# A hybrid decoder layer on one core: 19 instead of 12 of the 22 gate and up pairs by Strassen's products, and the decay differences made by ACT instead of POOL

## The chip, the core and the metric

The kernel runs on one core of one Trainium2 chip. Its engines work beside each other, each through its own list of instructions in the order in which they stand: TensorE (PE, with its weight loads shown apart as PEld), VectorE (DVE), ScalarE (ACT), GpSimd (POOL), and SyncE (SP), which here only issues DMAs. An instruction that waits for another engine or for a DMA holds up everything that stands behind it on its own engine. The metric is the time of one execution on the device in microseconds (us); lower is better. Three executions of the kernel before took 1591.46, 1591.48 and 1591.81 us; the median is 1591.48 us.

## What is computed

One decoder layer on 512 tokens of width 1024, in float32. The reference, cut to what the change touches:

```python
def swiglu(u, w_gate_up, w_down):
    gate, up = jnp.split(u @ w_gate_up, 2, axis=-1)
    return (jax.nn.silu(gate) * up) @ w_down

# per layer
h = h + 0.5 * swiglu(rmsnorm(h, ffn1_norm), ffn1_w_gate_up, ffn1_w_down)      # D_FF = 2816
...                       # short convolution, Mamba-2 SSD, gates, cross attention
h = h + 0.5 * swiglu(rmsnorm(h, ffn2_norm), ffn2_w_gate_up, ffn2_w_down)

# in the SSD part, per group of 8 heads and per chunk of 128 tokens
seg = acs[..., :, None] - acs[..., None, :]            # acs: running sum of dt * a
decay = jnp.exp(jnp.where(causal, seg, -jnp.inf))
y_diag = jnp.einsum('bcgls,bcgkls,bcsgkp->bclgkp', cb, decay, x)
```

## The kernel before

**Number format.** A matmul operand is kept as two parts that PE can multiply, `hi` (a rounded copy, made by ACT, line 103) and `lo` (what is left over, made by DVE, line 104). A product of two such operands is three matmuls for each 128 rows of the inner dimension: hi by hi, lo of the activations, lo of the weights. The third of every three matmuls therefore reads the weights' `lo`.

**The two feed-forward parts.** `ffn` runs at the start of the layer and again at its end. Its 2816 gate and 2816 up columns make 22 pairs `ct` = 0 to 21: 128 gate columns and 128 up columns each, with 1 MB of weights. They are worked off in blocks of eight (pairs 0 to 7, 8 to 15, 16 to 21). After each block come eight down projections (`job`, lines 130 to 132), one for each 128 columns of the model's width; these take the block's results `s` as their operands.

A pair is made in one of two ways. `plain` does 48 matmuls of 512 columns. The other way takes the pair as a 2 by 2 block product (gate and up against the two halves of the inner dimension, the two halves of the tokens on the other side) and does it with Strassen's seven products instead of eight: 84 matmuls of 256 columns. It needs sums of weight blocks, made anew for each pair, and sums of token blocks (`token_sums`, tiles `tq`, `th`, `tl`), made once in each of the two parts, behind pair 1. Which way a pair goes is decided by `seven(ct)`, line 47: before, for 4, 5, 7, 8, 10, 11, 13, 14, 16, 17, 19 and 20, so that never more than two such pairs follow one another.

Such a pair has a first half, `seven_a`, and a second, `seven_b`. `seven_a(n + 1)` is written ahead of `seven_b(n)`, so PE does first half, first half, second half, first half, second half, and so on. In `seven_a` the weights arrive in two transfers, `ca` (tile `wr`, three buffers) and `db` (two buffers). DVE adds blocks into `sa` (lines 278, 279), into `wr` itself (282) and `sb` (285); ACT and DVE split `sa` into `wh`, `wl` and the changed `wr` into `xh`, `xl` (two buffers). PE does four products: two from `sa` into the psum tile B, two from `wr` into A. ACT and DVE then copy and add halves of B (lines 290, 291) and of A (294, 295) into `ev`. In `seven_b` the split `sb` gives one product, the split `db` two; then DVE puts the results together (306, 307, 311, 312), ACT does the silu (247), DVE the product (251), and both split it into `sh`, `sl` for the down projections. A buffer of `db` is free for the transfer of the pair after next when its own split has been made (`xl<-db`, line 104).

**The SSD part.** For each of 32 heads a tile `m` (128 by 512) is filled by a DMA that repeats one head's row of `acs` on all partitions; then comes the difference with the column of `acs`, clamped on one side (lines 522 to 525), `exp` (526), and DVE's product with `cb` (527). PE takes it in line 539. Two heads at a time make one step of `ssd_out`.

**What sets the order.** The code is written in the order above, and a scheduler in the building of the program then puts each engine's instructions into one fixed order, so that an edit at one place can move instructions elsewhere. That order is what the engines follow.

Of the kernel before, what the change touches and what calls it, by code (L numbers as in the profile page):

```python
# [22 lines left out]
AF = mybir.ActivationFunctionType  # L23
ALU = mybir.AluOpType
AX = mybir.AxisListType

P = 128
# [14 lines left out]
NC = 4  # L42
# [3 lines left out]

def seven(ct):

    return ct >= 4 and ct % 3 != 0


COL = {}
# [10 lines left out]
def layer(ctx: ExitStack, tc: tile.TileContext, a, out):  # L63
    nc = tc.nc
    V, S, G, TE = nc.vector, nc.scalar, nc.gpsimd, nc.tensor
# [15 lines left out]
    def ps(tag="pj"):  # L81
        return psp.tile([P, T], F32, tag=tag, name=nm(tag), bufs=PJ if tag == "pj" else 8 - PJ)
# [16 lines left out]
    def pc(name, i):  # L99
        return prm[:, COL[name] + i:COL[name] + i + 1]  # L100
# [87 lines left out]
    def ffn(gname, wgu, wd, fin=None):  # L188
# [126 lines left out]
        for b0 in range(0, KF, SB):  # L315
            b1 = min(KF, b0 + SB)
            wait = None
            for ct in range(b0, b1):
                if seven(ct):
                    nxt = seven_a(ct)  # L320
                    if wait is not None:
                        seven_b(*wait)
                    wait = nxt
                else:
                    p = plain(ct)
                    if ct == 0:
                        r = rms(h, D, wk)
                    plain_out(ct, *p)
                    if wait is not None:
                        seven_b(*wait)  # L330
                        wait = None
                if ct == 1:
                    token_sums()
# [37 lines left out]
    def proj(ct):  # L371
        p = ps()
        job(p, win[ct], u)
        return p
# [9 lines left out]
    with tc.tile_pool(name="mx", bufs=1, reuse_waits="tile") as mx:  # L384

        def mt(tag, bufs, shape=(P, T), dt=F32):
            return mx.tile(list(shape), dt, tag=tag, name=nm(tag), bufs=bufs)
# [7 lines left out]
        for c in range(NC):  # L395
# [4 lines left out]
        dt, acs, dte, eend = (keep[:, i, :] for i in range(4))  # L400
# [3 lines left out]
                        in0=ptr[:, 0:P].rearrange("p (c h) -> p h c", c=NC),  # L404
                        in1=dtb[:, 0, :].rearrange("p (h c) -> p h c", c=NC), op=ALU.add)
# [107 lines left out]
        def ssd_out(g, ct, xs, cb, xdt, prev):  # L513
            yg = []
            for i in range(4):
                h0 = 8 * g + 2 * i
                ms = []
                for hh in range(2):
                    m = mt("m", MB)
                    DQ.dma_start(out=m, in_=acd_h[h0 + hh].partition_broadcast(P))  # L520
                    m4 = m.rearrange("p (c l) -> p c l", c=NC)
                    G.tensor_tensor(out=m4, in0=m4,
                                    in1=acs[:, (h0 + hh) * NC:(h0 + hh + 1) * NC].unsqueeze(2)
                                    .to_broadcast([P, NC, P]), op=ALU.subtract)
                    S.activation(out=m, in_=m, func=AF.Relu, scale=-1.0)
                    S.activation(out=m, in_=m, func=AF.Exp, scale=-1.0)
                    V.tensor_tensor(out=m, in0=m, in1=cb, op=ALU.mult)
                    ms.append(m)
                ea = mt("ea", 2)
                for hh in range(2):  # L530
                    DQ.dma_start(out=ea[64 * hh:64 * hh + 64, :],
                                 in_=acd_h[h0 + hh].partition_broadcast(64))
                S.activation(out=ea, in_=ea, func=AF.Exp)
                yd = ps("ss")
                for c in range(NC):
                    cs = slice(c * P, (c + 1) * P)
                    for hh in range(2):
                        q0 = (2 * i + hh) * 64
                        TE.matmul(yd[64 * hh:64 * hh + 64, cs], xdt[c][:, q0:q0 + 64], ms[hh][:, cs],  # L539
                                  start=True, stop=True)  # L540
                yo = ps("ss")
                for c in range(1, NC):
                    cs = slice(c * P, (c + 1) * P)
                    TE.matmul(yo[:, cs], prev[c - 1][:, i * P:(i + 1) * P], ct[:, cs],
                              start=True, stop=True)
                V.tensor_tensor(out=ea[:, P:], in0=yo[:, P:], in1=ea[:, P:], op=ALU.mult)
                y = mt("yg", 4)
                V.scalar_tensor_tensor(out=y, in0=xs[i], scalar=pc("ssm_d", 4 * g + i), in1=yd,
                                       op0=ALU.mult, op1=ALU.add)
                V.tensor_tensor(out=y[:, P:], in0=y[:, P:], in1=ea[:, P:], op=ALU.add)  # L550
                yg.append(y)
            return yg
# [16 lines left out]
        for g in range(NG):  # L569
            bt, ct, xs = nxt  # L570
            cb, xdt, prev = ssd_state(g, bt, ct, xs)
            yn = norm_y(g, ssd_out(g, ct, xs, cb, xdt, prev), zs)
            if g < NG - 1:
                nxt = ssd_in(g + 1)
                zs = gate_z(g + 1)
            else:
                sgb = []
                for k in range(KD):
                    p = proj(72 + k)
                    t = mt("xs", 8)  # L580
                    V.tensor_tensor(out=t, in0=p, in1=r, op=ALU.mult)
                    S.activation(out=t, in_=t, func=AF.Sigmoid)
                    sgb.append(t)
            for k in range(KD):
                p = ps()
                job(p, a["w_os"][k][:, g * 512:(g + 1) * 512], yn)
                if g == 0:
                    S.copy(out=yb[k], in_=p)
                else:
                    V.tensor_tensor(out=yb[k], in0=p, in1=yb[k], op=ALU.add)  # L590
                if g == NG - 1:
                    V.tensor_tensor(out=yb[k], in0=yb[k], in1=sgb[k], op=ALU.mult)

    with tc.tile_pool(name="mb", bufs=1, reuse_waits="tile") as mb:
        def wt(tag, bufs, dt=F32):
            return mb.tile([P, T], dt, tag=tag, name=nm(tag), bufs=bufs)
# [14 lines left out]
        for k in range(KD):  # L611
            pcg, pv, pb = proj(8 + k), proj(16 + k), proj(k)
            c = wt("c", 2)
# [29 lines left out]
        for k in range(KD):  # L643
            p = ps()
# [5 lines left out]
    with tc.tile_pool(name="xa", bufs=1, reuse_waits="tile") as xa:  # L650
        kT, vm = [], []
        with tc.tile_pool(name="xn", bufs=1, reuse_waits="tile") as xm:
# [6 lines left out]
            for k in range(KD):  # L659
                p = ps()  # L660
# [26 lines left out]
        with tc.tile_pool(name="xo", bufs=1, reuse_waits="tile") as xo:  # L687
# [86 lines left out]
            for k in range(KD):  # L774
                p = ps()
# [142 lines left out]
```

## Time and profile before

| | |
|---|---|
| median of three executions | 1591.48 us |
| the profiled execution, as timed | 1592.54 us |
| its span in the profile | 1590.8 us |
| instructions in the span | 20744 |
| PE, DVE, ACT, POOL busy, share of the span | 98%, 66%, 46%, 3% |

The profiled execution took 1.06 us more than the median; 1.7 us of it lie outside the span. The page gives each engine's busy time, the span in 40 slices, the chain of work that ended last, and groups of instructions by line. A matmul's duration in it is modelled and overlaps the next, so what a matmul costs is read from the distance between two starts. In a row of the timeline the columns are the start, the duration, the engine, the line, the operation, what it writes and reads, and in brackets the idle time before it and what ended that.

### The profile page before, as it was taken

To read this page: it belongs to the slowest core of one execution; us is meant where nothing else is said; L and a number is where in the kernel's file an instruction comes from. 1 tells how busy PE (TensorE), PEld (TensorE's weight loads), DVE (VectorE), ACT (ScalarE), POOL (GpSimd) and SP (SyncE) were. 2 spreads that over 40 slices of the span, in tenths; PEclk is the share of its full clock that TensorE was granted. 3 is DMA by queue.
4 is the path that set the end of the run, shared out by engine and by line. 5 is a ranking of instruction groups with operands and counts; after the bars stand their busy time and mean duration, and the time that the engine had idled before them with its cause. 6 is when DMAs were issued, how large, how long until landed. Compare 5 with 4: busy or idle time off the path is not lost.

```text
span 1590.8 us, 20744 instructions
## 1 busy us (share of the span) xinstructions
PE 1557.4 (98%) x8253; PEld 1318.0 (83%) x8253; DVE 1056.0 (66%) x1502; ACT 733.7 (46%) x1008; POOL 52.7 (3%) x54
## 2 busy tenths in 40 slices
PE   7999999999989999899999999999999999999997
PEld 6888988987778777787888888888888898998986
DVE  6856856777684877958565544565556876666765
ACT  7432433445768593765332233344344642342343
POOL 0000000002020200201000000000000000000000
PEclk9999999999999999999999999999999999999999
DMA  5432333245242423323242322235204233233221
GB/s 196 133 93 93 98 112 100 66 132 188 93 133 80 138 75 117 122 93 108 78 146 93 105 94 93 95 105 185 93 27 130 83 120 107 93 95 111 86 62 71
DMA packets 53920, 168.70 MB, mean 106 GB/s; under 512 B 6320, under 2 KB 6832, under 8 KB 53824
## 3 DMA queue, kind: packets, MB, share of 16 engines
q1 hardware_dynamic: 51952, 161.03, 31.8%
q0 software_dynamic: 1584, 5.31, 0.9%
q8 instruction: 64, 1.05, 0.3%
q10 hardware_dynamic: 288, 1.05, 0.2%
q14 instruction: 32, 0.26, 0.1%
HBM read 163.10 MB, written 4.26 MB: 105 GB/s over the span
## 4 chain that ended last, share of the span: by engine, by line
PE 55%; DVE 2%; issue 1%; ACT 1%; DMA 0%; DVEq 0%; ACTq 0%
PE pj L132 12%; PE pj L131 12%; PE pj L130 12%; PE pj L212 5%; PE pj L214 5%; PE pj L215 5%; DMA ea<-acd 0%; PE pj L676 0%; PE pj L678 0%; PE pj L677 0%; PE ss L539 0%; DVE wl L104 0%; PE ss L758 0%; ACT wh L103 0%; PE ss L721 0%
## 5 line engine op out<-in xcount | busy, mean ns | idle before, releaser
L103 ACT CAST wh<-wr 128x1024 fp32r<-128x1024 f32 (+2 forms) x250 | 243.6, 975 | 479.9 <-PE pj L131 332.2
L104 DVE TENSOR_TENSOR wl<-wr,wh 128x1024 fp32r<-128x1024 f32 (+2 forms) x250 | 282.0, 1129 | 112.6 <-ACT wh L103 111.0
L130 PE MATMUL pj<-uh,wh 128*128 128x512 f32 (+1 forms) x712 | 281.2, 395 | 0.0
L132 PE MATMUL pj<-uh,wl 128*128 128x512 f32 (+1 forms) x712 | 280.4, 394 | 0.0
L131 PE MATMUL pj<-ul,wh 128*128 128x512 f32 (+1 forms) x712 | 279.5, 393 | 0.0
L212 PE MATMUL pj<-uh,wh 128*128 128x512 f32 (+1 forms) x416 | 153.3, 369 | 8.3 <-ACT wh L103 7.1
L132 PEld LDWEIGHTS pj<-uh,wl 128*128 128x128 f32 (+1 forms) x712 | 133.9, 188 | 29.0 <-issue 0.7
L130 PEld LDWEIGHTS pj<-uh,wh 128*128 128x128 f32 (+1 forms) x712 | 133.8, 188 | 28.6 <-issue 0.9
L131 PEld LDWEIGHTS pj<-ul,wh 128*128 128x128 f32 (+1 forms) x712 | 134.0, 188 | 27.8
L214 PE MATMUL pj<-ul,wh 128*128 128x512 f32 (+1 forms) x416 | 152.4, 367 | 0.0
L215 PE MATMUL pj<-uh,wl 128*128 128x512 f32 (+1 forms) x416 | 151.9, 366 | 0.0
L130 PE MATMUL pj<-sh,wh 128*128 128x512 f32 x346 | 135.3, 391 | 0.1
L131 PE MATMUL pj<-sl,wh 128*128 128x512 f32 x346 | 135.1, 390 | 0.2
L132 PE MATMUL pj<-sh,wl 128*128 128x512 f32 x346 | 134.8, 390 | 0.0
L212 PEld LDWEIGHTS pj<-uh,wh 128*128 128x128 f32 x416 | 78.6, 189 | 22.6 <-ACT wh L103 7.1
L214 PEld LDWEIGHTS pj<-ul,wh 128*128 128x128 f32 x416 | 79.0, 190 | 13.1 <-DVE ul L140 0.5
L215 PEld LDWEIGHTS pj<-uh,wl 128*128 128x128 f32 x416 | 78.5, 189 | 12.8 <-DVE wl L104 0.2
L131 PEld LDWEIGHTS pj<-sl,wh 128*128 128x128 f32 x346 | 65.0, 188 | 14.5 <-DVE sl L104 1.5
L130 PEld LDWEIGHTS pj<-sh,wh 128*128 128x128 f32 x346 | 65.0, 188 | 14.0 <-ACT sh L103 0.9
L132 PEld LDWEIGHTS pj<-sh,wl 128*128 128x128 f32 x346 | 65.0, 188 | 13.4
L352 DVE SCALAR_TENSOR_TENSOR dn<-pj,r 128x512 f32<-128x512 f32 x47 | 32.4, 690 | 57.2 <-PE pj L132 56.9
L381 DVE SCALAR_TENSOR_TENSOR cv<-cx,prm,cv 128x511 f32<-128x511 f32 (+2 forms) x72 | 62.1, 866 | 3.4 <-ACT cv L378 3.1
(278 smaller groups left out, 3088.6 us busy)
## 6 DMA issues: line engine op xcount, KB each, us to landing
wr<-in_w_in SPq DMA_DIRECT2D x80, 512.0 KB, 3.2
wr<-in_w_gu SPq DMA_DIRECT2D x63, 512.0 KB, 3.8
wr<-in_w_d SPq DMA_DIRECT2D x32, 512.0 KB, 3.5
db<-in_w_gu SPq DMA_DIRECT2D x24, 512.0 KB, 3.8
m<-acd SPq DMA_DIRECT2D x32, 256.0 KB, 3.9
wr<-in_w_os SPq DMA_DIRECT2D x32, 256.0 KB, 3.1
wr<-in_w_d SPq DMA_DIRECT2D x16, 384.0 KB, 3.2
ea<-acd SPq DMA_DIRECT2D x32, 128.0 KB, 4.4
```

Of the source, the lines that this page charges most:

```text
L103: S.copy(out=hi, in_=src)
L104: V.tensor_tensor(out=lo, in0=src, in1=hi, op=ALU.subtract)
L130: TE.matmul(pt, hi[:, s_], xh, start=(k == 0), stop=False)
L131: TE.matmul(pt, hi[:, s_], xl, start=False, stop=False)
L132: TE.matmul(pt, lo[:, s_], xh, start=False, stop=(k == nk - 1))
L212: TE.matmul(pt, hi[:, c], xh, start=start and k == 0, stop=False, skip_group_check=True)
L214: TE.matmul(pt, hi[:, c], xl, start=False, stop=False, skip_group_check=True)
L215: TE.matmul(pt, lo[:, c], xh, start=False, stop=stop and k == 3, skip_group_check=True)
L352: V.scalar_tensor_tensor(out=dn, in0=pd, scalar=0.5, in1=r, op0=ALU.mult, op1=ALU.mult)
L381: V.scalar_tensor_tensor(out=acc[:, d:], in0=x[:, :T - d], scalar=pc(wname, j0 + j), in1=acc[:, d:], op0=ALU.mult, op1=ALU.add)
```

## The change

```diff
-    return ct >= 4 and ct % 3 != 0
+    return ct >= 3
...
                     DQ.dma_start(out=m, in_=acd_h[h0 + hh].partition_broadcast(P))
-                    m4 = m.rearrange("p (c l) -> p c l", c=NC)
-                    G.tensor_tensor(out=m4, in0=m4,
-                                    in1=acs[:, (h0 + hh) * NC:(h0 + hh + 1) * NC].unsqueeze(2)
-                                    .to_broadcast([P, NC, P]), op=ALU.subtract)
-                    S.activation(out=m, in_=m, func=AF.Relu, scale=-1.0)
+                    for c in range(NC):
+                        col = (h0 + hh) * NC + c
+                        S.activation(out=m[:, c * P:(c + 1) * P], in_=m[:, c * P:(c + 1) * P],
+                                     func=AF.Relu, scale=-1.0, bias=acs[:, col:col + 1])
                     S.activation(out=m, in_=m, func=AF.Exp, scale=-1.0)
```

In each of the two feed-forward parts, pairs 3, 6, 9, 12, 15, 18 and 21 go over to the block products: 38 pairs in all instead of 24. Behind the plain pairs 0, 1 and 2 no plain pair is left, and the block products now come in unbroken rows of 5, 8 and 6 pairs. The second edit does the difference inside the activation, by its bias, in four instructions of 128 columns each; POOL does no arithmetic in the SSD part any more. Lines behind 522 stand one lower in the changed file.

The first place is on DVE, in the first feed-forward part, where the token sums end and the first block products begin. It is one piece of the difference (`tq`, `tl` are token sums; `wr_89`, `wr_92` are the weights of pair 3 before, `wr_87`, `db_88` those of pair 3 now, `wr_98`, `db_99` those of pair 4 before; `pj_76`, `pj_77` the psum tiles of plain pair 2).

```order
 L238 SCALAR_TENSOR_TENSOR tq_73_364<-tq_73_364,ug_72_361 128x256
-L104 TENSOR_TENSOR wl_91_447<-wr_89_445,wh_90_446 128x1024
-L104 TENSOR_TENSOR wl_94_477<-wr_92_475,wh_93_476 128x1024
+L278 TENSOR_TENSOR sa_89_447<-wr_87_443,db_88_444 128x512
+L279 TENSOR_TENSOR sa_89_447<-wr_87_443 128x512
 L104 TENSOR_TENSOR tl_75_370<-tq_73_364,th_74_369 128x1024
-L278 TENSOR_TENSOR sa_100_517<-wr_98_513,db_99_514 128x512
+L282 TENSOR_TENSOR wr_87_443<-wr_87_443,sa_89_447 128x512
+L104 TENSOR_TENSOR wl_91_451<-sa_89_447,wh_90_450 128x1024
 L268 TENSOR_TENSOR gt_84_435<-pj_77_374,r_41_241 128x512
```

Where DVE split the weights of plain pair 3 it now makes the sums of a block-product pair.

The second place is also on DVE, in the second block of the first feed-forward part. Before, from the split of pair 10's `db` (tile `db_237`) on; `ev_257`, `xl_280` belong to pair 11, `wl_273` to plain pair 12, `sa_287`, `db_286` to pair 13, `sa_298` to pair 14, `xx_262` to pair 10:

```order
L104 TENSOR_TENSOR xl_261_1592<-db_237_1442,xh_260_1591 128x2x512
L295 TENSOR_TENSOR ev_246_1485<-pj_244_1459,ev_246_1485 128x256
L306 TENSOR_TENSOR xx_262_1631<-ev_246_1485 128x256
L104 TENSOR_TENSOR wl_273_1677<-wr_271_1675,wh_272_1676 128x1024
L291 TENSOR_TENSOR ev_257_1558<-pj_256_1533,ev_257_1558 128x256
L278 TENSOR_TENSOR sa_287_1773<-wr_285_1769,db_286_1770 128x512
L279 TENSOR_TENSOR sa_298_1846<-wr_296_1842 128x512
L282 TENSOR_TENSOR wr_285_1769<-wr_285_1769,sa_287_1773 128x512
L295 TENSOR_TENSOR ev_257_1558<-pj_255_1532,ev_257_1558 128x256
L104 TENSOR_TENSOR xl_280_1718<-db_248_1515,xh_279_1717 128x2x512
L307 TENSOR_TENSOR xx_262_1631<-pj_245_1460,ev_246_1485 128x512
```

In the change, from the row ahead of the split of pair 10's `db` (tile `db_253`) on; `ev_281` belongs to pair 11, `xx_286` and `gt_287` to pair 10, `sa_292`, `db_291` to pair 12, `sa_311` to pair 13:

```order
L291 TENSOR_TENSOR ev_281_1735<-pj_280_1710,ev_281_1735 128x256
L104 TENSOR_TENSOR xl_285_1769<-db_253_1563,xh_284_1768 128x2x512
L306 TENSOR_TENSOR xx_286_1808<-ev_262_1606 128x256
L295 TENSOR_TENSOR ev_281_1735<-pj_279_1709,ev_281_1735 128x256
L307 TENSOR_TENSOR xx_286_1808<-pj_261_1581,ev_262_1606 128x512
L312 TENSOR_TENSOR gt_287_1811<-xx_286_1808,r_41_241 128x256
L311 TENSOR_TENSOR gt_287_1811<-pj_260_1580,r_41_241 128x256
L278 TENSOR_TENSOR sa_292_1824<-wr_290_1820,db_291_1821 128x512
L279 TENSOR_TENSOR sa_311_1953<-wr_309_1949 128x512
L251 SCALAR_TENSOR_TENSOR gt_287_1811<-xx_286_1808,gt_287_1811 128x512
L104 TENSOR_TENSOR wl_294_1828<-sa_292_1824,wh_293_1827 128x1024
```

The addition for the pair after next (line 278) stood ahead of the gathering of the pair in hand (307) before, with a plain pair still to come on PE; now it stands behind it (307, 312, 311), and no plain pair comes between.

The third place is on ACT in the SSD part, at the third step of the first group of heads (`m_647`, `m_648` before, `m_703`, `m_704` now, are its two tiles). Before:

```order
L378 ACTIVATE cv_682_4078<-cx_681_4076,prm_69 128x512
L525 ACTIVATE m_647_3926<-m_647_3926 128x512
L526 ACT_TABLE_LOAD
L526 ACTIVATE m_647_3926<-m_647_3926 128x512
L525 ACTIVATE m_648_3932<-m_648_3932 128x512
```

Now:

```order
L378 ACTIVATE cv_738_4507<-cx_737_4505,prm_69 128x512
L523 ACTIVATE m_703_4347<-m_703_4347,keep_3801 128x128 x4
L523 ACTIVATE m_704_4355<-m_704_4355,keep_3801 128x128
L525 ACT_TABLE_LOAD
L525 ACTIVATE m_703_4347<-m_703_4347 128x512
```

The clamp that followed POOL's difference is now four instructions that do both.

## The prediction

> **What bounds the kernel now.** I read the page first: busy time, the granted clock, the chain that ended last.
>
> ```profile
> PE 1557.4 (98%) x8253; PEld 1318.0 (83%) x8253; DVE 1056.0 (66%) x1502; ACT 733.7 (46%) x1008; POOL 52.7 (3%) x54
> PEclk9999999999999999999999999999999999999999
> PE 55%; DVE 2%; issue 1%; ACT 1%; DMA 0%; DVEq 0%; ACTq 0%
> ```
>
> PE works nearly all the time, at nearly full clock in every slice, and the chain runs through PE. So a matmul saved is time saved, as long as PE does not wait for what it gets in exchange. Next the view of waits, for PE alone:
>
> ```profile
> PE ss L539 <- DVE m L527: 8.3, 4, 2.7
> PE pj L212 <- ACT wh L103: 7.1, 1, 7.1
> PE ss L158 <- DVE sq L154: 4.6, 3, 1.7
> ```
>
> Columns: us in total, times, the longest. These three are 20.0 us; the rest of that answer adds 6.2. The 7.1 us is the start of the program, the two others lie in the SSD part. Inside the feed-forward blocks PE waits for nothing. There it is the bound, with DVE next (columns: us of the stretch, busy us and instructions of PE, PEld, DVE, ACT, POOL):
>
> ```profile
> 30.00:97.40 67.40, 67.39 (x421) 60.44 (x420) 55.93 (x83) 36.97 (x50) 0.00 (x0) 1.00 0.33 102
> 140.50:222.00 81.50, 81.50 (x566) 75.83 (x565) 56.71 (x83) 34.88 (x49) 0.00 (x0) 1.00 0.32 99
> ```
>
> In the first block DVE is already busy for 55.9 of 67.4 us.
>
> **What a pair is worth on PE.** Distances between starts in the timeline of the first block:
>
> ```profile
> 71.80 0.40 PE L212 MATMUL pj<-uh,wh 128*128 128x512 f32 x1
> 82.70 0.28 PE L212 MATMUL pj<-uh,wh 128*128 128x256 f32 x1
> 86.91 0.29 PE L212 MATMUL pj<-th,wh 128*128 128x256 f32 x1
> 92.44 0.39 PE L130 MATMUL pj<-sh,wh 128*128 128x512 f32 x1
> ```
>
> Plain pair 6 takes 82.70 - 71.80 = 10.90 us. The second half of pair 5 takes 4.21 and the first half of pair 7 takes 5.53: 9.74 for a pair. Fourteen pairs change over: 14 x 1.16 = **16.2 us less** work for PE.
>
> **What DVE must do for it.** Steps from start to start in the same block:
>
> ```profile
> 69.47 0.69 DVE L282 TENSOR_TENSOR wr<-wr,sa 128x512 f32<-128x512 f32 x1
> 70.08 1.22 DVE L104 TENSOR_TENSOR xl<-db,xh 128x1024 fp32r<-128x1024 f32 x1
> 71.22 0.42 DVE L295 TENSOR_TENSOR ev<-pj,ev 128x256 f32<-128x256 f32 x1
> 71.55 0.68 DVE L104 TENSOR_TENSOR wl<-sb,wh 128x512 fp32r<-128x512 f32 x1
> ```
>
> 512 columns cost 0.61, 1024 cost 1.14, 256 cost 0.33. A block-product pair has 8, 3 and 5 of these: 9.95 us, some 10.3 with a tenth where one hangs on the one before. That is more than PE's 9.74; a plain pair (two of 1024, three of 512) needs 4.1. With a plain pair in every three DVE had slack. In rows of 5, 8 and 6 it has none, and worse, its order makes a loop.
>
> **The loop.** By the order shown with the change, line 278 for pair n + 2 needs `db`, whose transfer needs the split of pair n's `db`, which stands beside line 291 of pair n + 1, which waits for PE's first products of pair n + 1. Before, a plain pair's 10.9 us on PE lay inside that loop; now nothing does. Its links:
>
> ```profile
> 59.29 0.28 PE L212 MATMUL pj<-uh,xh 128*128 128x256 f32 x1
> 59.65 0.36 ACT L290 COPY ev<-pj 128x256 f32<-128x256 f32 x1
> 168.05 1.22 DVE L104 TENSOR_TENSOR xl<-db,xh 128x1024 fp32r<-128x1024 f32 x1
> 169.29 0.33 SPq L275 DMA_DIRECT2D db<-in_w_gu  x1
> 173.07 0.69 DVE L278 TENSOR_TENSOR sa<-wr,db 128x512 f32<-128x512 f32 x1 [0.85 <-DMA db<-in_w_gu]
> L103 ACT CAST wh<-sa 128x1024 fp32r<-128x1024 f32 x24 | 25.3, 1054 | 64.6 <-PE pj L214 39.0 <-PE pj L131 18.9 <-DVE sa L279 6.6
> L104 DVE TENSOR_TENSOR wl<-sa,wh 128x1024 fp32r<-128x1024 f32 x24 | 29.3, 1222 | 9.3 <-ACT wh L103 9.3
> ```
>
> From the third matmul of a pair's first half, the first to read `wl`, to the end of its B part: 22 steps of 0.115 (5.53 us over 48), 2.5 us. PE's next part starts at 59.29, ACT's copy at 59.65 and ends 0.72 behind. Line 291: 0.33 to 0.42, 0.45 with the handing over. `xl<-db`: 1.22. From the transfer's issue (169.29) to line 278 (173.07): 3.8, and DVE did wait for it. Line 278: 0.69. The cast: 1.05. `wl`: 1.22. Three handings over: 0.2. Sum 2.5 + 0.72 + 0.45 + 1.22 + 3.8 + 0.69 + 1.05 + 1.22 + 0.2 = **11.9 us** until the next pair's third matmul can start. Lines 312, 311 and 282 stand between 278 and `wl`, longer than the cast by 0.3; at some pairs 279 or 251 stands there too, 0.6 each. I take 12.4 for a turn, with ends 11.9 and 13.1 (both of the 0.6). Against 9.74 a turn loses 2.7 (2.2 to 3.4).
>
> How many turns: in a row of n pairs the first two are made ready under the down projections, where DVE idles; the third finds its transfer just in time; from the fourth on each is a full turn. Rows of 5, 8, 6 give 2 + 5 + 3 = 10, in two feed-forward parts 20: **54 us more** (44 to 68).
>
> **The ends of the rows.** The last pair of a row has no first half behind it to cover its `db` split, which waits for a buffer that PE frees with the half before: cast 1.05 + `xl` 1.14 + 0.25 = 2.44 against 1.41 + 0.23 of covering matmuls, 0.8 us, six times: 4.8 (0 to 7). The third pair of blocks two and three: 0.3, four times: 1.2 (0 to 4).
>
> **The start of the first block.**
>
> ```profile
> 56.46 0.28 PE L212 MATMUL pj<-th,wh 128*128 128x256 f32 x1
> 42.48 0.43 DVE L238 SCALAR_TENSOR_TENSOR tq<-tq,ug 128x256 f32<-128x256 f32 x1
> ```
>
> Without plain pair 3 the first block product is due at 56.46 - 10.90 = 45.56. DVE ends line 238 at 42.82; behind it stand 278, 279, a `tl`, 282 and the `wl` (first order piece), 3 x 0.61 + 2 x 1.14 = 4.1: `wl` is there at 46.9, the third matmul due at 45.8: 1.1. Up to the next pair's `wl` DVE has eleven instructions, 8 of 512 columns, 2 of 1024, 1 of 256: 7.5, so 54.4 against 46.9 + 5.53 = 52.4: 2.0. Third pair: `xl<-db` of the first ends 3.8 later (58.2), its transfer lands at 62.0, four of 512 and a `wl` more give 65.6, due 54.4 + 9.74 = 64.1: 1.5. Together 4.6, in both parts **9 us** (4 to 16), taking the second part to begin as the first.
>
> **The SSD part.**
>
> ```profile
> 440.64 5.25 POOL L522 TENSOR_TENSOR m<-m,keep 128x512 f32<-128x512 f32 x4 [38.74 <-DMA m<-acd]
> 441.71 0.63 ACT L525 ACTIVATE m<-m 128x512 f32<-128x512 f32 x1 [6.29 <-POOL m L522]
> 442.36 1.28 ACT L526 ACT_TABLE_LOAD   x1
> 443.66 0.63 ACT L526 ACTIVATE m<-m 128x512 f32<-128x512 f32 x1
> 444.91 1.52 DVE L381 SCALAR_TENSOR_TENSOR cv<-cx,prm,cv 128x509 f32<-128x509 f32 x1
> 446.35 0.68 DVE L527 TENSOR_TENSOR m<-m,cb 128x512 f32<-128x512 f32 x1
> ```
>
> PE's wait of 2.7 us at the third step: the four tiles land, POOL takes 1.31 each, then come clamp, table load, `exp`, and DVE's 527, which stands behind DVE instructions that take 1.52 where the same lines take 0.7 elsewhere:
>
> ```profile
> L381 DVE SCALAR_TENSOR_TENSOR cv<-cx,prm,cv 128x509 f32<-128x509 f32 x24 | 20.1, 839 | 0.1
> L381 DVE SCALAR_TENSOR_TENSOR cv<-cx,prm,cv 128x511 f32<-128x511 f32 x24 | 18.4, 767 | 3.1 <-ACT cv L378 3.1
> L525 ACT ACTIVATE m<-m 128x512 f32<-128x512 f32 x32 | 19.4, 621 | 25.6 <-POOL m L522 25.6
> L294 ACT COPY ev<-pj 128x256 f32<-128x256 f32 x24 | 8.8, 366 | 2.0 <-PE pj L215 2.0
> ```
>
> An activation of 128 columns is nowhere in the trace; by the line through 512 (0.62) and 256 (0.37) it takes 0.24, bounded by 0.16 (a quarter of 0.62) and 0.37. Four make 0.96 (0.62 to 1.5) in place of POOL's 1.31 and ACT's 0.62, about 1 us shorter, and the doubled DVE instructions all fall while POOL works. Of the four waits (8.3 us) I take back **6**. Best, the 4.6 us of `sq` behind them go in part too: 12. Worst, ACT now stands where POOL stood and waits for the landing, with weight casts behind it that PE needs: 4 us lost (0.25 at each of 16 steps). ACT's own work grows by 32 x 0.34 = 11 us, less the table loads that its new order drops (20 to 13 in front of `exp`, 1.28 each); ACT is busy for 46% of the span, so PE is the cover, and if ACT were late it would show as casts that PE waits for.
>
> **Sum**, on the profiled execution (1592.54, that is 1.06 above the median of the three): -16.2 + 54 + 4.8 + 1.2 + 9 - 6 = +46.8, so 1639.3, and 1638 on the median. The ends together: 1592.5 - 16.2 + 44 + 4 - 12 = 1612 and 1592.5 - 16.2 + 68 + 7 + 4 + 16 + 4 = 1675.
>
> **Rivals.** (a) *The transfer is hidden and the products pay.* If `db` lands before line 278 is reached, and the DVE chain behind it fits under PE, no turn forms: 1592.5 - 16.2 - 6 = 1570. For it: DVE waited for `db` only 0.85 us in the row above, and in all before, a transfer stood in no path of PE. Against it: there a plain pair gave 10.9 us of cover. It decides at a turn of 10.1 us, where 20 turns lose 7 and starts and ends 15, as much as the products and the SSD part give. The links sum to 11.9, and only one of them, the 3.8, could shrink. (b) *DVE's sum alone is the pace*, the chain being hidden: a turn of 10.3 loses 0.56, 20 lose 11: 1592.5 - 16.2 + 11 + 15 - 6 = 1596. (c) *PE's clock falls in the waits.* The first matmuls of the program go at half pace:
>
> ```profile
> 11.75 0.63 PE L212 MATMUL pj<-uh,wh 128*128 128x512 f32 x1
> 12.17 0.63 PE L214 MATMUL pj<-ul,wh 128*128 128x512 f32 x1
> 451.54 0.40 PE L131 MATMUL pj<-ul,wh 128*128 128x512 f32 x1
> 451.77 0.39 PE L132 MATMUL pj<-uh,wl 128*128 128x512 f32 x1
> ```
>
> 0.42 from start to start against 0.23 soon after the wait of 2.7 us. If each turn's wait brought the slow pace back, the 2.5 us of PE in the turn would be 5: 20 x 2.5 = 50 more, 1689. The Trainium skill, page "TensorE: Matmul & The Clock Gate", section "What's actually happening", says that the clock is halved after an idle window of about 3.4 us. By that rule the trace agrees: 2.7 us of idling left the pace whole, and turns that wait 2.7 us would stay below the window, but not by much.
>
> **How the numbers follow.** Forecast 0.78, (a) 0.07, (b) 0.10, (c) 0.05. The likeliest is the forecast, so 1638. Its own ends with (c)'s lower reaches give a range of 1608 to 1676, which leaves out (a), (b) and the upper part of (c). A measurement of this kernel tells a change of about 0.2% (3.2 us) from none. Faster: (a) and a little of (b), 0.09. Same: 0.05, of (b). Slower: 0.86.
>
> **What would show it.** Right, if in the middle of a row the starts of first halves lie 12 to 13 us apart in PE's timeline, PE's waits list `wh` and `wl` of `sa` (lines 212, 214, 215) at some 50 us, and `db` transfers are issued right behind `xl<-db`. If the distance is 9.7, (a) holds; if it is 10.3 with DVE never idle, (b); if matmuls of 256 columns stand 0.23 apart, (c). In the SSD part PE's wait for `m` should fall from 8.3 to some 2 us, and lines 381, 550 and 556 should lose their long instances. The forecast is wrong if line 278 starts well before 3.8 us after the issue, or if what one turn loses is made up in the next.

## The result

The changed kernel takes **1651.68 us** (median of four, 1645.66 to 1654.57), the kernel before 1591.47 beside it: a ratio of 1.0374 (95% interval 1.0348 to 1.0400), 60 us more. The profiled execution took 1650.58 us, with a span of 1648.5. The forecast was 1638 with a range of 1608 to 1676.

Page of the changed kernel: busy time, granted clock by slices, the chain that ended last.

```profile
PE 1578.9 (96%) x8757; PEld 1352.5 (82%) x8757; DVE 1114.2 (68%) x1656; ACT 760.5 (46%) x1145; POOL 10.4 (1%) x22
PEclk9999999999999999999999999999999999989999
PE 78%; DVE 12%; DMA 6%; ACT 2%; issue 1%; SPq 0%; DVEq 0%; ACTq 0%
```

DVE's share of the chain went from 2% to 12%, that of the DMAs from 0% to 6%. PE is busy for 21.5 us longer although it has 16.2 us less to do, and the mean granted clock fell from 0.995 to 0.981. PE's waits, in the columns of before:

```profile
PE pj L212 <- ACT wh L103: 40.0, 23, 7.0
PE pj L215 <- DVE wl L104: 7.4, 15, 0.8
PE pj L212 <- ACT xh L103: 4.3, 8, 1.0
PE pj L132 <- DVE wl L104: 3.5, 1, 3.5
PE ss L538 <- DVE m L526: 1.9, 3, 1.4
```

The first three are new, but for the 7.0 at the program's start: 44.7 us in the feed-forward parts. The fourth is new too, once in the SSD part; the wait for `m` fell from 8.3 to 1.9, and the 4.6 for `sq` are gone. DVE in turn waits for the transfer that the loop was drawn around:

```profile
DVE sa L278 <- DMA db<-in_w_gu: 35.2, 18, 3.0
```

Before, that row read 5.3 us in 6 waits. By PE's timeline the loss sits where it was forecast: the first feed-forward part, to the start of the last matmul of its down projections, is 30.2 us longer (389.79 against 359.55), the second, from its first product to PE's last matmul, 34.9 (391.7 against 356.8). The SSD part, from the transposes of `dt` (line 396) to PE's last matmul on `yn`, is 8.6 shorter (422.6 against 431.1).

One turn of the loop, from the timeline of the second block (from `db`'s split for one pair to that for the next):

```profile
208.53 1.22 DVE L104 TENSOR_TENSOR xl<-db,xh 128x1024 fp32r<-128x1024 f32 x1
209.81 0.33 SPq L275 DMA_DIRECT2D db<-in_w_gu  x1
213.67 0.69 DVE L278 TENSOR_TENSOR sa<-wr,db 128x512 f32<-128x512 f32 x1 [2.44 <-DMA db<-in_w_gu]
214.39 1.04 ACT L103 CAST wh<-sa 128x1024 fp32r<-128x1024 f32 x1 [3.62 <-DVE sa L278]
215.49 0.38 PE L212 MATMUL pj<-th,wh 128*128 128x256 f32 x1 [0.92 <-ACT wh L103]
216.14 1.22 DVE L104 TENSOR_TENSOR wl<-sa,wh 128x1024 fp32r<-128x1024 f32 x1
217.42 0.39 PE L215 MATMUL pj<-th,wl 128*128 128x256 f32 x1
221.64 0.28 PE L215 MATMUL pj<-uh,xl 128*128 128x256 f32 x1
221.84 0.37 ACT L290 COPY ev<-pj 128x256 f32<-128x256 f32 x1 [2.09 <-PE pj L215]
222.25 0.42 DVE L291 TENSOR_TENSOR ev<-pj,ev 128x256 f32<-128x256 f32 x1 [1.34 <-ACT ev L290]
222.59 1.22 DVE L104 TENSOR_TENSOR xl<-db,xh 128x1024 fp32r<-128x1024 f32 x1
```

Issue to line 278 takes 3.86 us, and each link stands in the place where the prediction put it. The turn is 14.1 us long. What is longer here than the sum of the links is one of them: the 22 steps from 217.42 to 221.64 take 4.2 us, not 2.5. Not every turn is bound by the transfer in the end. In twelve of the 20 turns line 278 waited for `db`. In the other eight it ran right behind line 307 or 311, which had waited for PE, as in the turn ahead of this one:

```profile
201.04 0.69 DVE L307 TENSOR_TENSOR xx<-pj,ev 128x512 f32<-128x512 f32 x1 [1.03 <-PE pj L215]
201.65 0.68 DVE L278 TENSOR_TENSOR sa<-wr,db 128x512 f32<-128x512 f32 x1
```

The granted clock in this block (us of the stretch, busy us and instructions of PE, PEld, DVE, ACT, POOL, then PEclk, the DMA share and GB/s):

```profile
176.45:190.52 14.07, 10.66 (x85) 10.00 (x85) 11.66 (x21) 5.99 (x10) 0.00 (x0) 1.00 0.25 76
190.52:203.47 12.95, 11.90 (x85) 11.28 (x85) 9.45 (x16) 4.83 (x8) 0.00 (x0) 0.87 0.24 82
203.47:215.49 12.02, 10.29 (x84) 9.87 (x85) 9.46 (x16) 5.24 (x9) 0.00 (x0) 1.00 0.29 89
215.49:229.50 14.01, 12.39 (x85) 11.62 (x85) 10.85 (x19) 5.36 (x9) 0.00 (x0) 0.88 0.24 75
229.50:246.27 16.77, 15.95 (x121) 15.74 (x121) 14.65 (x22) 9.81 (x14) 0.00 (x0) 0.90 0.50 150
```

Each stretch begins with a pair's first half; the last one holds the two second halves that end the row, and is no turn. In three of the five the clock is down for a part of the time. But the longest turn of the block, the first one shown, ran at full clock. So two theories had to be told apart: the loop with the transfer in it, which makes waits by which the clock then falls, or the clock as a cause of its own.

### The profile page after: what moved, and what is told of

It is laid out like the page before. It is cut to its first block, busy times and chain, and to the rows that moved or that the text cites. A ratio compares the mean times of both kernels' runs of the same rounds, so it can differ in the third digit from the quotient of the medians.

```text
span 1648.5 us, 21859 instructions
## 1 busy us (share of the span) xinstructions
PE 1578.9 (96%) x8757; PEld 1352.5 (82%) x8757; DVE 1114.2 (68%) x1656; ACT 760.5 (46%) x1145; POOL 10.4 (1%) x22
## 3 DMA queue, kind: packets, MB, share of 16 engines
q0 software_dynamic: 1584, 5.31, 0.9%
q10 hardware_dynamic: 288, 1.05, 0.2%
## 4 chain that ended last, share of the span: by engine, by line
PE 78%; DVE 12%; DMA 6%; ACT 2%; issue 1%; SPq 0%; DVEq 0%; ACTq 0%
PE pj L132 19%; PE pj L131 19%; PE pj L130 19%; DMA db<-in_w_gu 5%; PE pj L215 5%; PE pj L212 5%; PE pj L214 4%; DVE wl L104 2%; DVE xl L104 2%; DVE sa L278 1%; PE ss L538 1%; DVE wr L282 1%; DMA ea<-acd 1%; DVE xx L307 1%; PE ss L489 1%
## 5 line engine op out<-in xcount | busy, mean ns | idle before, releaser
L132 PE MATMUL pj<-uh,wl 128*128 128x512 f32 (+1 forms) x712 | 279.4, 394 | 3.5 <-DVE wl L104 3.5
L130 PE MATMUL pj<-uh,wh 128*128 128x512 f32 (+1 forms) x712 | 280.6, 394 | 0.0
L131 PE MATMUL pj<-ul,wh 128*128 128x512 f32 (+1 forms) x712 | 279.6, 393 | 0.0
L212 PE MATMUL pj<-th,wh 128*128 128x256 f32 x304 | 95.3, 313 | 33.1 <-ACT wh L103 33.1
L215 PE MATMUL pj<-th,wl 128*128 128x256 f32 x304 | 95.6, 314 | 6.7 <-DVE wl L104 6.6
L214 PE MATMUL pj<-tl,wh 128*128 128x256 f32 x304 | 92.7, 305 | 0.0
L212 PE MATMUL pj<-uh,xh 128*128 128x256 f32 x304 | 86.3, 284 | 4.5 <-ACT xh L103 4.3
L215 PE MATMUL pj<-uh,xl 128*128 128x256 f32 x304 | 85.6, 282 | 0.0
L214 PE MATMUL pj<-ul,xh 128*128 128x256 f32 x304 | 85.5, 281 | 0.0
L212 PE MATMUL pj<-th,xh 128*128 128x256 f32 x304 | 84.8, 279 | 0.0
```

The lines of the kernel that those rows point to most:

```text
L130: TE.matmul(pt, hi[:, s_], xh, start=(k == 0), stop=False)
L131: TE.matmul(pt, hi[:, s_], xl, start=False, stop=False)
L132: TE.matmul(pt, lo[:, s_], xh, start=False, stop=(k == nk - 1))
L212: TE.matmul(pt, hi[:, c], xh, start=start and k == 0, stop=False, skip_group_check=True)
L214: TE.matmul(pt, hi[:, c], xl, start=False, stop=False, skip_group_check=True)
L215: TE.matmul(pt, lo[:, c], xh, start=False, stop=stop and k == 3, skip_group_check=True)
```

## The experiments

Each kernel was timed beside the kernel before; the first four, the second four and the last four on one chip each.

**1 and 2. The two edits apart.** One kernel takes only the new set of pairs, the other only ACT's decay differences.

```diff
 # pairs only: from the kernel before
-    return ct >= 4 and ct % 3 != 0
+    return ct >= 3
 # decay only: from the changed kernel
-    return ct >= 3
+    return ct >= 4 and ct % 3 != 0
```

> Only the set of pairs changes (19 of 22), the decay differences stay on POOL. The theory, that the feed-forward parts lose and the SSD part gains each by itself: the changed kernel's 1651.7 plus the 8.6 us by which its SSD stretch became shorter, 1660 us (1656 to 1664), and the SSD stretch as before, 431 us. The rival, that the two edits act on each other or that the SSD gain comes from elsewhere: 1652, with the SSD stretch at 423.

> Only the decay differences move to ACT, the 12 pairs stay. The theory: before less 8.6, 1583 us (1580 to 1586), PE's waits for m down from 8.3 to about 2 us. The rival: the part pays only in the changed kernel, 1591.

Pairs only: 1657.81, a ratio of 1.0403 (1.0363 to 1.0442). Decay only: 1582.69, 0.9933 (0.9914 to 0.9952). Against 1593.13 of before on that chip this is 64.7 more and 10.4 less, together 54.2; the two edits together gave 60 and, in a second measurement below, 56. They nearly add up, so the whole loss comes from the pairs. In one respect the first run was not as expected: its SSD stretch is 426.9 us in the trace, not 431, though POOL still makes the differences. PE waits there nearly as before (8.8 us for `m`, 3.4 for `sq`). Most of the 4 us is the clock, which was down in this part before and is not in the first run. Before:

```profile
440.00:480.00 40.00, 35.88 (x172) 28.51 (x171) 35.54 (x47) 30.29 (x42) 10.66 (x8) 0.91 0.41 122
```

Pairs only:

```profile
440.00:480.00 40.00, 36.87 (x204) 28.79 (x204) 29.19 (x39) 24.92 (x35) 5.48 (x4) 1.00 0.30 99
```

Over the whole part PE is busy for 414.2 us instead of 417.4, at the same work, and idle for 12.7 instead of 13.8. Waits of the kernel with the decay edit alone:

```profile
PE pj L132 <- DVE wl L104: 3.5, 1, 3.5
PE ss L538 <- DVE m L526: 2.4, 4, 1.0
```

The wait for `m` falls, `sq` is gone from the list, and the one new wait of 3.5 comes with the decay edit, not with the pairs.

**3. A third buffer for `db`,** with the room for it taken elsewhere.

```diff
-            ws = [fp.tile([P, 1280], F32R, tag=t, name=nm(t), bufs=2) for t in ("xh", "xl")]
+            ws = [fp.tile([P, 1184], F32R, tag=t, name=nm(t), bufs=2) for t in ("xh", "xl")]
-            db = fp.tile([P, 1024], F32, tag="db", name=nm("db"), bufs=2)
+            db = fp.tile([P, 1024], F32, tag="db", name=nm("db"), bufs=3)
-            s4 = fp.tile([P, 512], F32, tag="sb", name=nm("sb"), bufs=2)
+            s4 = fp.tile([P, 512], F32, tag="sb", name=nm("sb"), bufs=1)
```

> The changed kernel with three buffers for db instead of two; the room is taken from sb (one buffer) and from the unused end of xh and xl (1184 columns instead of 1280). The theory of the loop: the transfer's 3.8 us leave it, a turn falls from 13.0 to between DVE's 10.3 and about 11.5, so 20 turns give back 30 to 54 us: 1598 to 1622, and starts of first halves lie under 11.5 us apart. Rival, that DVE's sum or the clock is the pace and the transfer is not: 1645 to 1655, distances still 13.

1576.29 us, 0.9895 (0.9872 to 0.9918): 75 us less than the changed kernel, below the 1598 to 1622 expected, and faster than the kernel before. The transfer of pair n + 3 now waits for the split of pair n, a whole pair earlier. Lines 278 and 307 in DVE's timeline (cut) and the window of four turns:

```profile
172.65 0.69 DVE L278 TENSOR_TENSOR sa<-wr,db 128x512 f32<-128x512 f32 x1 [0.16 <-DMA db<-in_w_gu]
...
182.73 0.69 DVE L278 TENSOR_TENSOR sa<-wr,db 128x512 f32<-128x512 f32 x1
...
186.54 0.69 DVE L307 TENSOR_TENSOR xx<-pj,ev 128x512 f32<-128x512 f32 x1
...
192.84 0.69 DVE L278 TENSOR_TENSOR sa<-wr,db 128x512 f32<-128x512 f32 x1
...
154.81:194.43 39.62, 39.41 (x338) 39.07 (x337) 38.56 (x63) 20.87 (x32) 0.00 (x0) 1.00 0.33 107
```

DVE's order is another one too: line 278 for the pair after next stands ahead of line 307 again, as it did before the change, so it no longer stands behind an instruction that waits for PE. What the earlier transfer does by itself and what this order does was not tried apart; run 8 tests the transfer without this order.

The window answers rival (b) as well. DVE is busy for 38.56 of 39.62 us, and its line 278 comes round in 10.1 us: with the transfer out of the way DVE's own sum is the next bound, as that rival priced it (10.3). But PE meets it only in the middle of a row of eight, probably because DVE works ahead under the down projections: three of this block's five turns are at PE's 9.72, two at 10.15 and 10.03.

**4. PE kept at work in its waits.** Sixteen matmuls, whose product is overwritten, ahead of the first half of each pair from the fourth of a row on.

```diff
             A, B = ps(), ps()
+            if ct % SB >= 3 and (ct >= SB or ct >= 6):
+                for k in range(16):
+                    TE.matmul(B[:, 0:H], u[k % 8][0][:, 0:P], u[k % 8][0][:, 0:H], ...)
             mm3(B[:, 0:H], w31, 512, tsum(0), True, True)
```

> The changed kernel with 16 more matmuls of 256 columns (1.84 us) at the head of the first half of every pair from the fourth of a row on, 20 times 16, whose product is overwritten: PE works in most of its wait, the links of the loop stay. The loop alone as the cause: the filling lies in the wait and the time stays, 1648 to 1660. The clock as part of the cause (the halved pace behind the waits): the clock stays up and what it cost is given back, 23 us by the granted clock of the whole span (0.981 of 1648.5 against 0.995 of 1590.8), so 1620 to 1635. If PE's own work were the bound: 20 x 1.84 = 37 more, 1689.

1643.11 us, 1.0306 (1.0282 to 1.0330), between the two expectations. The cores' view (span, mean granted clock) of the changed kernel and of this one:

```profile
core 0: 1648.5 us, clock 0.981
...
core 0: 1642.6 us, clock 0.994
```

The clock is back where it was before the change, and 37 us of extra matmuls cost nothing: they lay in the waits. Yet the time falls by 9 us only (6 against the second measurement in 9), not by 23. The turns stay at 12.7 us. The clock is mainly a follower. The changed kernel's own turns say the same: nine of the 20 have a granted clock of 0.79 to 0.88 and take 13.34 us on average, the other eleven, at 0.96 to 1.00, take 12.73; that is 5.5 us in all. Of the 9 us a part may be the scheduler's, since the order on DVE differs from the changed kernel's in places. So the clock costs some 5 to 9 us.

**5. Rows of three.** The changed kernel, with a plain pair behind every three.

```diff
-    return ct >= 3
+    return ct >= 4 and ct % 4 != 3
```

> ACT makes the decay differences, db has two buffers, and a plain pair follows every three pairs of block products (pairs 4-6, 8-10, 12-14, 16-18, 20-21: 14 of 22). The theory, by which a turn is late only from the fourth pair of a row on: 4 more block-product pairs than the 12 in two parts, 4 x 1.16 = 4.6 less than the decay edit alone (1582.7): 1578 (1574 to 1584). Rival, that a turn is late from the third pair on: 8 third pairs at some 3.2 more, 1604.

1585.47 us, 0.9951 (0.9934 to 0.9968), just above the 1574 to 1584 expected: not told apart from the decay edit alone (0.9933, 0.9914 to 0.9952). In the trace the feed-forward parts do what the theory says: PE waits for no `wh`, `wl` or `xh` there, but for the program's start, and they are 2.6 and 2.2 us shorter than with 12 pairs, 4.8 against the 4.6 expected. No turn is late at the third pair. Between the down projections and the end of the SSD part 3.1 us are lost again; PE waits 2.4 us for `btok` and 1.4 for `xe` there (line 489), which it does not with the decay edit alone. The traces are 2.0 us apart in the end. The pairs' worth is shown in its place; for the whole kernel it is too little to measure.

**6. The room made and not used,** the control for 3: two buffers for `db`, the two other lines of that diff kept.

> The changed kernel with the room made and not used: one buffer for sb, 1184 columns for xh and xl, two buffers for db. The theory of the loop: no link of it is touched, 1652 (1644 to 1660). Rival, that a part of what the run with three buffers won came from this and from the order that it makes: under 1640.

1642.34 us, 1.0313 (1.0288 to 1.0338), between the two expectations, so it was run again at the end.

**7. The third buffer with the 12 pairs of before.**

> Three buffers for db and the decay on ACT, but the 12 pairs of before. The theory: with a plain pair in every three no turn was late, so the third buffer gives nothing: 1583 (1579 to 1587), and the distance to the run with three buffers and 19 pairs (1576.3) is what 14 pairs are worth without the loop, 16.2 less the start of the first blocks. Rival, that the third buffer itself is the gain: 1570 or less.

1585.55 us, 0.9955 (0.9940 to 0.9969). The third buffer gives nothing where no row is longer than two, as expected; the gain in 3 belongs to the long rows. Run 3 with its 19 pairs is 9.3 us below this one. In the traces its two feed-forward parts are 6.8 and 6.3 us shorter, 13.1 of the 16.2 that 14 pairs save on PE; most of the rest is lost at the start of the first blocks.

**8. `db` transferred twice,** the second transfer behind the first.

```diff
             nc.sync.dma_start(out=db, in_=wgu[ct][:, 1024:])
+            nc.sync.dma_start(out=db, in_=wgu[ct][:, 1024:])
```

> The changed kernel with the transfer of db made twice, the second behind the first into the same tile: the transfer's link doubles from 3.8 to some 7.3. The theory of the loop: 3.5 more in each of 20 turns and at the four third pairs of blocks two and three, 70 to 84 more than the changed kernel, 1722 to 1736. Rival, that the transfer is not a link (DVE's sum, or the clock): 1650 to 1665.

1744.23 us, 1.0951 (1.0924 to 1.0977), 92.6 more than the changed kernel, where 70 to 84 were expected. The link in its timeline (lines behind 275 are one higher here):

```profile
216.63 1.22 DVE L104 TENSOR_TENSOR xl<-db,xh 128x1024 fp32r<-128x1024 f32 x1
217.91 0.33 SPq L275 DMA_DIRECT2D db<-in_w_gu  x1
221.68 0.33 SPq L276 DMA_DIRECT2D db<-in_w_gu  x1
225.49 0.69 DVE L279 TENSOR_TENSOR sa<-wr,db 128x512 f32<-128x512 f32 x1 [0.57 <-DMA db<-in_w_gu]
```

Issue to addition is 7.58 us instead of 3.86, and the mean turn is 16.45 instead of 13.01: what the link gains, 3.7, arrives in the turn almost whole, 3.4. That is what a link on the loop does. The match is not exact, though: the clock fell to 0.951, and PE's 22 steps take 4.3 us on average here instead of 3.3, while other waits of the loop shrank. The 20 turns are 68.9 of the 92.6; third pairs (2.1 to 2.7 more each) and the first block of each part (3.5 and 3.7 more) are another 16.5.

**9 and 10. The changed kernel and the control again,** on one chip.

> The changed kernel once more, beside the next run on the same chip: 1652 (1645 to 1658). It is here to tell whether the 9 us between it and the run with the room made and not used are real.

> The room made and not used, once more. If sb's single buffer and the order of instructions that comes with it are worth something by themselves, 1642 and 8 to 11 below the changed kernel beside it; if the first distance was scatter between chips and runs, both within 4 of each other.

1648.81 us, 1.0352 (1.0333 to 1.0372), and 1642.27, 1.0306 (1.0286 to 1.0326). The distance, 9 us the first time, is 6.5 now: it is there, but smaller than expected. One buffer less for `sb` and the order made with it are worth some 6 to 9 us (the control's fourth pairs start 9.7 to 10.5 us behind the third, not 10.8 to 11.8, in the second and third blocks). In the second block of the first control line 278 stands ahead of line 307 at first, as in run 3, but with two buffers it still waits for `db`: 1.46 and 1.88 us, at turns of 10.35 and 11.85 us. So of the 75 us in 3 the third buffer, with the order that the scheduler made for it, has 66 (1642.3 to 1576.3).

**11 and 12. The better version,** three buffers for `db`, with 18 and with 19 pairs.

```diff
-    return ct >= 3
+    return ct >= 4
```

> Three buffers for db, and pair 3 plain again (18 pairs). The theory, that block products from pair 3 on start before DVE has their sums: pair 3 as block products won 1.16 of PE's work and cost the waits at the start of the first block, 0.35 + 0.42 + 0.63 + 0.72 = 2.1 us there: 1 us less in each part, 2 us below the run with 19 pairs beside it (1574), with no wait before the first block products. Rival, that these waits move on to the next pairs: 2.3 more (1578.6), and waits as long, later.

> Three buffers for db and 19 pairs, once more, beside the run with 18: 1576 (1573 to 1580), faster than the kernel before by 0.7 to 1.3%.

18 pairs: **1573.50 us**, 0.9875 (0.9858 to 0.9893). 19 pairs: 1576.92, 0.9893 (0.9872 to 0.9914). Both beat the kernel before and the changed one; between the two the times do not decide, as the intervals overlap. In the trace pair 3 as a plain pair leaves no wait in front of the first block products, and the two feed-forward parts are 1.8 and 1.2 us shorter than with 19.

Turns by PE's timeline, the mean of the 20 distances between first halves from the third pair of a row on:

```
kernel                     mean turn, us   granted clock   time, us
changed                        13.01           0.981        1651.7
PE kept at work                12.74           0.994        1643.1
db transferred twice           16.45           0.951        1744.2
three buffers for db            9.79           0.995        1576.3
```

## Why the prediction was right, and where it was off

**The mechanism held.** The loop was drawn with the transfer as the one link that could shrink. Taking that link out removed the loss (3, 12; DVE's order changed with it), doubling it added its length to the turn (8), shorter rows made no turns (5), and without long rows the buffer did nothing (7). Rival (a) is out: DVE waited for `db` 18 times. The Trainium skill, page "Perfetto Trace Analysis", section "Optimization Strategy", says that a gap which keeps its size over a stretch, on the engine that should be full, can mean too little room for the next tile. This case agrees: at first halves 11.2 to 14.4 us apart, 4 KB in each partition were worth 66 us.

**The turn, 12.4, was 13.01,** near the upper end of 11.9 to 13.1. Single turns run from 11.18 to 14.38. Twenty turns cost 260.1 - 20 x 9.74 = 65.3 us, not 54. PE's link, 22 steps at 0.115, was too short: it takes 2.5 to 2.7 us in eleven turns, but in the nine with a lower clock the steps are 0.21 to 0.23 for a while, and it takes 3.6 to 4.7. By the eleven turns at 12.73, the clock is about half of the 11.3 us more. The transfer, put at 3.8, takes 4.3 from issue to line 278 on average of the twelve turns in which line 278 waits for it. And the prediction drew one way round only: in the other eight turns line 278 stands behind line 307 or 311, which waits for PE's second half.

**Rival (c), the clock, had 0.05 and 50 us.** It is true in part: the clock does fall, in nine of the 20 turns, and costs some 5 to 9 us. The prediction reasoned that a wait of 2.7 us leaves the pace whole. That was a misreading: the row that it shows at 451.54 starts 4.4 us behind that wait, and in the trace of before the clock was down between the two:

```profile
447.80:451.20 3.40, 3.40 (x22) 2.79 (x21) 2.04 (x3) 3.37 (x6) 0.00 (x0) 0.54 0.00 0
```

So the small chance of (c) rested on a wrong reading, and that the loss stayed small is not to the reasoning's credit. In the changed kernel the clock fell behind shorter waits too, as the rows at the end of the second block show:

```profile
229.50 0.39 PE L212 MATMUL pj<-th,wh 128*128 128x256 f32 x1 [1.16 <-ACT wh L103]
229.73 0.28 PE L214 MATMUL pj<-tl,wh 128*128 128x256 f32 x1
230.83 0.38 PE L215 MATMUL pj<-th,wl 128*128 128x256 f32 x1 [0.82 <-DVE wl L104]
231.05 0.28 PE L212 MATMUL pj<-th,wh 128*128 128x256 f32 x1
...
231.63 0.37 PE L215 MATMUL pj<-th,wl 128*128 128x256 f32 x1
231.80 0.42 PE L212 MATMUL pj<-th,wh 128*128 128x256 f32 x1
```

**The ends of the rows, 4.8 us of stalls, did not come.** PE stands nowhere in the last second halves: from 97.53 to 105.94 in the first block, 8.41 us, two times 4.2. The stretch from a row's last first half to the next block is longer all the same, by 11.8 us in the six rows (58.70, 60.31 and so on against 57.55 in run 12), because that first half itself runs slow or waits. So the term stood in the wrong place, and at 4.8 (0 to 7) it was too small.

**The third pairs, 1.2 us, were nothing:** their starts lie 15.34 us behind the row's first, against 15.32 with three buffers.

**The start of the first block, 9 us, was 5.0.** First to third first half take 18.68 us in the first part and 16.84 in the second, against 5.53 + 9.74 = 15.27. Only the first part was worked out; the second, taken to be the same, begins better.

**Fourteen pairs at 1.16** can be seen in run 5, where nothing covers them: 4.8 for four pairs against 4.6.

**The SSD part, -6, was -8.6.** The wait for `m` went from 8.3 to 1.9, that for `sq` from 4.6 to nothing, and one of 3.5 is new; PE's idle time in the part fell from 13.8 to 6.5 us. As forecast, DVE's long instances are gone: line 381 on 510 columns took 993 ns before (24 instructions), and takes this now:

```profile
L381 DVE SCALAR_TENSOR_TENSOR cv<-cx,prm,cv 128x510 f32<-128x510 f32 x24 | 17.9, 744 | 0.1
```

How much of the gain is the shorter chain and how much DVE free of POOL was not tried apart.

**The sum.** -16.2 + 65.3 + 11.8 + 5.0 - 8.6 = 57.3, beside a profiled execution that is 58.0 longer. The forecast's +46.8 was short by the turns (11.3) and the ends of the rows (7.0), and too high by the start (4.0), the SSD part (2.6) and the third pairs (1.2). That these errors cancel in part is luck.

## What to carry to other kernels

Before more work goes onto an engine that has slack on average, write down the loop from one iteration's buffer release to the next iteration's use of it: if its links sum to more than the bounding engine's work for an iteration, the loop sets the pace, and one more buffer for the tile that closes it is the first thing to try. A mixture of two kinds of iteration can owe its speed to the slower kind, which covers what the faster kind leaves open, so read the loop without that cover. Double the suspected link: if the period grows by as much, the link is on the loop.

## What the hardware did that was not expected

**The clock fell without a long idle time.** In the rows above PE was idle for 1.16 and 0.82 us with two matmuls between, and 0.8 us after it had resumed its steps went to twice their length. The stretch ahead of that moment and the one behind it:

```profile
228.20:231.60 3.40, 1.43 (x10) 1.07 (x9) 3.40 (x7) 3.20 (x5) 0.00 (x0) 1.00 0.00 0
231.60:235.00 3.40, 3.40 (x18) 3.40 (x17) 2.71 (x4) 1.92 (x3) 0.00 (x0) 0.51 0.22 37
```

PE was busy for 1.43 of the 3.40 us ahead. The longest idle time of this block was 3.16. The Trainium skill, page "TensorE: Matmul & The Clock Gate", section "What's actually happening", has a window of about 3.4 us that runs free of the kernel. The trace agrees in so far as the halved pace lasts for about 3.4 us here, and as nearly the same waits are followed by it in one turn and not in another (1.16 and 0.82 at 229.50; 1.05 and 0.81 at 203.47, where the clock stayed at 1.00), but the stretch ahead of it was not idle throughout.

**An activation of 128 columns costs more than a line through larger ones gives.** A group of before:

```profile
L407 ACT ACTIVATE m<-m 128x128 f32<-128x128 f32 x1 | 0.3, 311 | 0.0
```

The group and one row of the changed kernel:

```profile
L523 ACT ACTIVATE m<-m,keep 128x128 f32<-128x128 f32 x128 | 42.1, 389 | 13.4 <-DMA m<-acd 13.4
...
440.07 1.27 ACT L523 ACTIVATE m<-m,keep 128x128 f32<-128x128 f32 x4
```

The prediction said that no activation of 128 columns was in the trace of before; lines 406, 407, 417 and 424 have one each, at 0.31 us, without the bias column that line 523 reads. With it one takes 0.389 us, above the bound of 0.37 that the prediction took from 256 columns (which `ev<-pj` reads from PSUM); four take 1.27, so one starts 0.29 behind the other, where 0.24 was assumed. The Trainium skill, page "VectorE: DVE Perf Modes", section "The TRN2 errata — SBUF-src ops pay a fixed extra latency per instruction", gives an activation from SBUF 224 cycles of 1.2 GHz beside one for each column, which makes an estimate of 0.29 us for 128; the trace agrees.

**Two kernels that differ in one tile's buffers and two tiles' spare columns differ by 6 to 9 us** (6, 10), though in both the transfer stays in the loop: at this size the scheduler's order is a term of its own, and a difference of some 0.5% between two builds is not yet a mechanism.
